# Shorter rows for the summing DMAs, fewer spilled partial sums and earlier table loads in a two-layer decoder trunk

## Chip, cores and metric

The kernel runs on one core of one Trainium2 chip. The metric is device time in microseconds (us) of one execution: the median of repeated runs. Beside the runs there is one execution under the hardware profiler, which gives the page and the trace that this document reads. Engines are named as the profile names them: PE is TensorE (matmuls; PEld its weight loads), DVE is VectorE, ACT is ScalarE, POOL is GpSimd, SP is SyncE, which issues most DMAs.

## The reference

A decoder trunk of two layers on 1024 tokens with a model width of 1024, all in float32. Each layer normalizes the tokens, projects them for four token mixers (latent attention with a rotary key, "a"; short gated convolution, "b"; causal pooling, "c"; sliding-window attention, "d"), normalizes each mixer's 256 outputs, joins them and projects them with `w_o` onto the residual; then comes a gated FFN of width 2816.

```python
for l in range(DEPTH):
    h = rmsnorm(x, attn_norm[l])
    proj = h @ w_in[l]
    (c_q, c_kv, k_r, g_b, g_c, u_conv, u_pool, q_sw, k_sw, v_sw) = jnp.split(proj, pts, axis=-1)
    y_a = mla_attention(c_q, c_kv, k_r, mla_q_norm[l], mla_kv_norm[l], w_uq[l], w_ukv[l], cos, sin)
    y_b = short_gated_conv(g_b, g_c, u_conv, conv_w[l])
    y_c = multiscale_pool(u_pool, pool_w[l], pool_scale[l])
    y_d = swa_sink_attention(q_sw, k_sw, v_sw, sinks[l], slopes)     # reshapes left out
    groups = jnp.stack([y_a, y_b, y_c, y_d], axis=2)
    gf = groups * lax.rsqrt(jnp.mean(groups * groups, axis=-1, keepdims=True) + RMS_EPS)
    mixed = gf.reshape(b, s, D_MIX) * mix_norm[l]
    x = x + mixed @ w_o[l]
    h2 = rmsnorm(x, ffn_norm[l])
    gate, up = jnp.split(h2 @ w_gate_up[l], 2, axis=-1)
    x = x + (jax.nn.silu(gate) * up) @ w_down[l]
return rmsnorm(x, final_norm)
```

## The kernel before

**Tiling.** Activations lie transposed: 128 channels on the partitions, 512 tokens (a half, `t` = 0 or 1) along the free dimension. Every float32 operand is split into a rounded high part and the rest (`split`, L285 to L293: a cast on ACT, L287 or L290, and a subtraction on DVE, L288 or L291), and a product is three matmuls (`mm3`, L270; all matmuls of this kind have line L276). A matmul of 128x512 starts every 0.227 us in the steady loops.

**Buffers.** `Slots` hands out 47 places of SBUF, each two halves of 128x512. A half is taken from the list of single free halves first, oldest first, else from the oldest free place. Which instruction reuses which half is thus fixed when the program is written out, and the reuse waits for the last reader, a DMA too. Small tiles have tags with their own buffers: `te` 2, `tn` 3, `tp` 3 (`tmp`, L186); PSUM has eight banks in four tags (`ps`, L180), and the tag "wide" goes round mm, s, mm, s, t, s, t.

**Order.** The framework orders the instructions of each engine at build time by its own model of the machine, so the trace does not show them strictly in the order of the code. Each engine then takes its list in order, and so does SP with the DMAs it issues.

**The stages of a layer.** First the projections: `project()` takes one weight tile (fetched one ahead by `ahead()`), makes two products of 24 matmuls, and steps the generator `dn_sums` twice. Window attention (`swa_unit`, transposes at L560), convolution and pooling run between them. Then come the query projections `cq`, `ckv`, and the rotary key, for which `rope_k` is loaded at L772 and multiplied on DVE, and `rope_q`, loaded at L790. Latent attention runs in eight steps over heads and halves (L1186 to L1240): `scores` (matmuls L890 to L892, exponentials L909 and L912), `mix_values` of the step before (transposes L944, matmuls L956, two small POOL memsets at L953), and 0, 3, 3, 3, 1, 1, 1, 1 parts of the output projection (`out_part`), which use mixers b, c and d alone.

**Partial sums.** A part (d, t) is output channels 128 d on and half t; OUT_PARTS goes through d = 0 to 7 with t = 1, then 0. `out_part` adds the residual, fetched by `fetch_x` (L1012). The first 13 parts are written to `xp` in HBM (L1000), and their half is freed; the last three stay. `out_last` reads the 13 back (L1084), adds mixer a's product (L1095), splits the result for the FFN, writes it to `xr` (L1098) and adds its squares to the norm `ss2` (L322, L324, L328).

**Sums of down-projection weights.** The FFN's down projection is done with seven products instead of eight (a Winograd form of Strassen's scheme), which needs sums of weight blocks. `dn_sums` makes them in HBM: per layer 16 plain copies (L159) and 16 DMAs that add onto them (L164, `accum_op`), 704 KB each, issued by POOL, each held back by `after_pe` until the last matmul written so far is done. The argument `max_dma_last_dim` bounds a DMA row.

**FFN start.** The first two gate/up columns are done plainly (`plain(f, u)`, u = 0 for t = 1): four products of 12 matmuls each, then gate times norm `r2[u]` on DVE, SiLU on ACT (L1292), times norm on POOL (L1293), and gate times up on DVE. The norm's matmul is L334 (`rnorm`: ACT L336 to L338, DVE L339 and L342). Between them `combine(j)` makes the sums of activations for the Strassen form, with four `tp` tiles (L1058, L1045, L1064, L1066) and four splits. From the third column on, `GateUp` loads a column's weights, sums blocks on POOL (L1128 to L1130), and splits them in `split1` to `split4`.

Of the kernel before, what the change touches and what calls it, by code (L numbers as in the profile page):

```python
# [33 lines left out]
HALVES = (1, 0)  # L34
OUT_PARTS = tuple((d, t) for d in range(NK) for t in HALVES)
N_U = 47
NG = NFF // 2


# [67 lines left out]
def trunk_kernel(ctx: ExitStack, tc: tile.TileContext, ins, out):  # L107
# [26 lines left out]
    act.preload_act_table_set("natural_log_exp_and_others")  # L134

    xs = dpool.tile([NK, P, S], F32, name="xs")
    xp = dpool.tile([NK, P, S], F32, name="xp")
    xr = dpool.tile([NK, P, S], F32, name="xr")
    ad = [dpool.tile([P, NG * HT], F32, name=f"ad{n}") for n in range(7)]

# [13 lines left out]
    def dn_sums(l):  # L154

        w = ins["w_dn"][l]
        for q, a, b in ((0, 2, 3), (2, 2, 0), (1, 0, 0), (3, 1, 1)):
            for m in range(NK // 2):
                after_pe(pool.dma_start(qd[q][m], qd[a][m] if q in (1, 3) else w[m, a]))  # L159
                yield  # L160
            for m in range(NK // 2):
                row = 4 * NG * P
                after_pe(
                    pool.dma_start(qd[q][m], w[m, b], accum_op=ALU.add, max_dma_last_dim=row)  # L164
                )
                yield

# [18 lines left out]
    def tmp(tag="te"):  # L186
        return tpool.tile([P, HT], F32, name=tag, tag=tag, bufs={"te": 2, "tn": 3, "tp": 3}[tag])
# [157 lines left out]
    def mul_to(o, a, b):  # L345
        dve.tensor_tensor(out=o, in0=a, in1=b, op=ALU.mult)  # L346
# [38 lines left out]
    for l in range(L):  # L385
# [344 lines left out]
            swa_some(2)  # L730
        R.free(sw)

        cq = [[None, None], [None, None]]
        sq_q = SumSq(2 * P)
        for m in range(2):
# [22 lines left out]
        for t in range(2):  # L758
            p = ps("mm")
            for k in range(NK):  # L760
                for n in range(2):
                    pe.matmul(
                        p,
                        wkr[:, k * P : (k + 1) * P],
                        R.ap(hh[k][t][n]),
                        start=k == 0 and n == 0,
                        stop=k == NK - 1 and n == 1,
                    )
            if t == 1:
                ahead()  # L770
            tk = F.half()
            sp.dma_start(F.ap(tk), ins["rope_k"][:, t * HT : (t + 1) * HT])  # L772
            mul_to(F.ap(tk), F.ap(tk), r_of(t))
            f = tmp()
            mul_to(f, p, F.ap(tk))
            F.free(tk)
            kr = half_split(f)
            p = ps("t")
            for n in range(2):
                pe.matmul(p, e_r, R.ap(kr[n]), start=n == 0, stop=n == 1)  # L780
                R.free(kr[n])
            for s in range(2):
                kb_[s][0][t], kb_[s][1][t] = R.half(), R.half()
                split(R.ap(kb_[s][0][t])[tl], R.ap(kb_[s][1][t])[tl], p[tl])
# [1 line left out]

        tq = []
        for t in range(2):
            s = F.half()
            sp.dma_start(F.ap(s), ins["rope_q"][:, t * HT : (t + 1) * HT])  # L790
            r = sq_q.rnorm(t)
            mul_to(F.ap(s), F.ap(s), F.ap(r))
            F.free(r)
            tq.append(s)
# [181 lines left out]

        x = [[None, None] for _ in range(NK)]

        def out_part(d, t, keep):
            next(sums, None)  # L980
            if t == HALVES[0]:
                out_w[:] = take()
# [11 lines left out]
            if t == HALVES[1]:  # L994
                ahead()
            dve.tensor_tensor(out=F.ap(s), in0=F.ap(s), in1=p, op=ALU.add)
            if keep:
                x[d][t] = s
            else:
                sp.dma_start(xp[d][:, t * HT : (t + 1) * HT], F.ap(s))  # L1000
                F.free(s)

        parts = deque(OUT_PARTS)
        coming = deque(OUT_PARTS)
# [7 lines left out]
                sp.dma_start(F.ap(s), src[:, t * HT : (t + 1) * HT])  # L1012
                residual.append(s)

        def out_some(n, keep=False):
            for _ in range(n):
                d, t = parts.popleft()
                out_part(d, t, keep)
                if d == NK - 1:
                    for g in "dcb":  # L1020
                        for c in range(2):
                            for s in mixed.pop((g, c, t)):
                                R.free(s)
# [54 lines left out]

        def out_last(t, ma):

            for d in range(NK):
                if x[d][t] is None:
                    x[d][t] = F.half()
                    sp.dma_start(F.ap(x[d][t]), xp[d][:, t * HT : (t + 1) * HT])  # L1084
            for d in range(NK):
                p = ps("wide")
                wh, wl = (R.ap2(i) for i in wa[d // 4])
# [157 lines left out]
            R.free(kb_[1][n][0])  # L1245
            R.free(va[n][1])
        ma0 = norm_a(0)
        out_some(len(parts), keep=True)
        out_last(HALVES[0], ma1)
        while ring:  # L1250
            ring_drop()
# [11 lines left out]
        def plain(f, u):  # L1263
# [4 lines left out]
            product(pg, blocks(w.s2, 0), hb[b[1]], False, True)  # L1268
            product(pu, blocks(w.s2, 1), hb[b[0]], True, False)
            product(pu, blocks(w.s1, 1), hb[b[1]], False, True)  # L1270
            if f == 0:
                r2.append(F.ap(ss2.rnorm(HALVES[u], tag="pv")))
            gate = tmp("tp")
            mul_to(gate, pg, r2[u])
            silu(gate, r2[u])
            acts[f].append(F.half())
            mul_to(F.ap(acts[f][u]), pu, gate)
            if u:
                for i in w.s1 + w.s2:
                    R.free_pair(i)  # L1280

        pending = None
        r2 = []

        def neg_mul(o, a, b):
            dve.scalar_tensor_tensor(  # L1286
# [106 lines left out]
        plain(0, 0)  # L1393
        combine(0)
        plain(1, 0)
        combine(1)
        plain(0, 1)
        w.sums()
        w.split1()
        w.split2()  # L1400
        combine(2)
        plain(1, 1)
        wn = GateUp(3)
        combine(3)
        for hl in hb[B12]:
            for i in hl:
                R.free(i)
# [306 lines left out]
```

## Time and profile before

| what | us |
|---|---|
| median of three runs | 2153.32 (2153.15 to 2154.82) |
| the profiled execution | 2153.01 |
| its span, first to last instruction | 2151.2 |
| DVE, ACT and POOL busy in the span | 1488.7, 989.8 and 430.2 |
| 0 to 340 us (layer 0, mixers): PE busy | 313.20 of 340 |
| 340 to 475 us (end of mixing, first FFN columns): PE busy | 129.76 of 135 |
| 475 to 520 us (third and fourth column): PE busy | 40.86 of 45 |
| 520 to 850 us (gate/up columns): PE busy | 330.00 of 330 |
| 850 to 1080 us (down projection): PE busy | 229.82 of 230 |
| 1080 to 1400, 1400 to 1540 and 1540 to 1580 us (the same in layer 1): PE busy | 300.58, 135.01 and 33.87 |

The granted PE clock is 0.986 over the span. A busy PE is not one at its peak, since matmuls overlap; what counts is the distance between their starts. On the DMA side, SP's queue moved 249.23 MB in 106,224 packets (33.2% of the time of the 16 DMA engines), and POOL's queue 46.19 MB in 5,664 packets (8.8%).

### The profile page before, as it was taken

Reading aid. Unit: us, or ns where it says so; the run is one execution under the profiler, and the core shown is the slowest. Engines: PE = TensorE matmul, PEld = TensorE weight load, DVE = VectorE, ACT = ScalarE, POOL = GpSimd, SP = SyncE. Lnnn points to the kernel's source line nnn. Section 1 sums busy time; section 2 is a strip of 40 time slices with the busy share of each in tenths; the row PEclk is TensorE's granted clock in tenths of the full one; section 3 lists DMA queues with packets and bytes.
Section 4 is the critical chain, followed back from the end, with each engine's and each line's share of the span. In section 5 each row is a group of like instructions: output and inputs, shape, how many; then the busy total and the mean of one; then the engine's idle time right before and its main releaser. Section 6 shows DMA issues by size and latency. Waiting matters only on the chain.

```text
span 2151.2 us, 26099 instructions
## 1 busy us (share of the span) xinstructions
PE 2073.8 (96%) x9418; PEld 1686.3 (78%) x9418; DVE 1488.7 (69%) x2417; ACT 989.8 (46%) x1716; POOL 430.2 (20%) x349
## 2 busy tenths in 40 slices
PE   8999889999999999999999998899999999999998
PEld 6777768687888888888888776677778888888887
DVE  6877958787666666655657888588876666675555
ACT  6446636663333334444433566366533333344442
POOL 0000000034535443000001000000353545410000
PEclk9999999999999999999999999999999999999999
DMA  4553453423232234866425444534223223267652
GB/s 176 138 153 100 125 152 124 162 80 111 85 127 85 107 113 142 291 239 201 149 86 144 125 106 133 138 121 149 82 90 122 94 103 116 81 222 267 214 183 89
DMA packets 112017, 297.08 MB, mean 138 GB/s; under 512 B 12672, under 2 KB 27008, under 8 KB 111376
## 3 DMA queue, kind: packets, MB, share of 16 engines
q1 hardware_dynamic: 106224, 249.23, 33.2%
q0 software_dynamic: 5664, 46.19, 8.8%
q8 instruction: 74, 1.21, 0.2%
q14 instruction: 55, 0.45, 0.1%
HBM read 231.40 MB, written 110.10 MB: 159 GB/s over the span
## 4 chain that ended last, share of the span: by engine, by line
PE 82%; DVE 7%; DMA 4%; ACT 3%; issue 2%; POOL 1%; SPq 0%; DVEq 0%; ACTq 0%; POOLq 0%
PE ps_mm L276 31%; PE ps_s L276 24%; PE ps_t L276 10%; PE ps_pv L276 8%; PE ps_pv L956 2%; PE ps_t L944 1%; DMA xp<-u 1%; DVE u L288 1%; PE ps_t L334 1%; PE ps_pv L572 1%; PE ps_s L890 1%; ACT u L287 1%; DVE u L291 1%; PE ps_t L560 1%; DVE u L328 1%
## 5 line engine op out<-in xcount | busy, mean ns | idle before, releaser
L276 PE MATMUL ps_mm<-u,u 128*128 128x512 f32 (+1 forms) x3394 | 839.3, 394 | 14.2 <-ACT u L290 11.1
L276 PEld LDWEIGHTS ps_mm<-u,u 128*128 128x128 f32 x3394 | 626.5, 191 | 142.1 <-ACT u L290 11.7
L276 PE MATMUL ps_s<-u,u 128*128 128x512 f32 x2652 | 632.3, 392 | 12.9 <-ACT u L287 5.9
L276 PEld LDWEIGHTS ps_s<-u,u 128*128 128x128 f32 x2652 | 498.5, 188 | 124.9 <-ACT u L287 6.8
L287 ACT CAST u<-u 128x1024 fp32r<-128x1024 f32 (+2 forms) x372 | 324.6, 897 | 428.8 <-PE ps_mm L276 130.5
L288 DVE TENSOR_TENSOR u<-u,u 128x1024 fp32r<-128x1024 f32 (+2 forms) x372 | 409.9, 1121 | 140.2 <-ACT u L287 115.5
L276 PE MATMUL ps_t<-u,u 128*128 128x512 f32 (+1 forms) x1146 | 260.3, 379 | 1.0 <-DVE u L1095 1.0
L276 PEld LDWEIGHTS ps_t<-u,u 128*128 128x128 f32 x1146 | 206.5, 188 | 43.6 <-issue 2.2
L1293 POOL TENSOR_TENSOR tp<-tp,u 128x512 f32<-128x512 f32 x88 | 132.7, 1507 | 398.3 <-ACT tp L1292 398.3
L276 PE MATMUL ps_pv<-u,u 128*128 128x512 f32 x744 | 176.4, 389 | 0.0
L276 PEld LDWEIGHTS ps_pv<-u,u 128*128 128x128 f32 x744 | 139.7, 188 | 29.0
L1292 ACT ACTIVATE tp<-tp 128x512 f32<-128x512 f32 x88 | 55.7, 633 | 148.1 <-DVE tp L346 147.7
L288 DVE TENSOR_TENSOR u<-ps_t,u 128x512 fp32r<-128x512 f32 (+4 forms) x136 | 78.3, 583 | 31.8 <-ACT u L287 30.8
L287 ACT CAST u<-ps_t 128x512 fp32r<-128x512 f32 (+4 forms) x136 | 67.0, 504 | 60.9 <-PE ps_t L944 30.6
L290 ACT ACTIVATE u<-u,par 128x512 fp32r<-128x512 f32 x100 | 70.1, 717 | 49.6 <-DVE u L1095 20.9
L1128 POOL TENSOR_TENSOR u<-u,u 128x512 f32<-128x512 f32 x40 | 62.6, 1565 | 128.1 <-PE ps_s L276 52.6
L346 DVE TENSOR_TENSOR tp<-tp,u 128x512 f32<-128x512 f32 x80 | 84.6, 1057 | 1.3
L1150 POOL TENSOR_TENSOR u<-u 128x512 f32<-128x512 f32 x40 | 69.0, 1725 | 58.2 <-DVE u L288 58.2
L291 DVE SCALAR_TENSOR_TENSOR u<-u,par,u 128x512 fp32r<-128x512 f32 x100 | 73.5, 760 | 8.6 <-ACT u L290 8.4
L164 POOL DMA_DIRECT2D qd<-in_w_dn x32 | 26.8, 942 | 260.8 <-PE ps_mm L276 80.0
L159 POOL DMA_DIRECT2D qd<-in_w_dn x16 | 7.9, 502 | 353.1 <-PE ps_t L276 289.6
L1286 DVE SCALAR_TENSOR_TENSOR u<-te,tp 128x512 f32<-128x512 f32 x40 | 29.8, 746 | 64.9 <-POOL tp L1293 64.9
(189 smaller groups left out, 2249.8 us busy)
## 6 DMA issues: line engine op xcount, KB each, us to landing
u<-in_w_gu SPq DMA_DIRECT2D x88, 512.0 KB, 3.6
ad<-u SPq DMA_DIRECT2D x154, 256.0 KB, 2.1
u<-ad SPq DMA_DIRECT2D x70, 512.0 KB, 5.3
qd<-in_w_dn POOLq DMA_DIRECT2D x48, 704.0 KB, 7.0
u<-qd SPq DMA_DIRECT2D x32, 512.0 KB, 4.9
u<-in_w_in SPq DMA_DIRECT2D x30, 512.0 KB, 3.5
u<-in_w_dn SPq DMA_DIRECT2D x24, 512.0 KB, 4.8
qd<-qd POOLq DMA_DIRECT2D x16, 704.0 KB, 4.7
```

The lines of the kernel that those rows point to most:

```text
L276: last_mm = pe.matmul(o, w, r, start=start and k == 0 and i == 0, stop=stop and k == n - 1 and i == 2, skip_group_check=again,)
L287: act.copy(hi, f)
L288: dve.tensor_tensor(out=lo, in0=f, in1=rd(hi), op=ALU.subtract)
L290: act.activation(hi, f, AF.Copy, scale=gain)
L291: dve.scalar_tensor_tensor(out=lo, in0=f, scalar=gain, in1=rd(hi), op0=ALU.mult, op1=ALU.subtract)
L346: dve.tensor_tensor(out=o, in0=a, in1=b, op=ALU.mult)
L956: pe.matmul(py[:, c0:], v_of(j, h), R.ap(s)[:, c0:], start=j == 0 and n == 0, stop=j == nj - 1 and n == 1,)
L1128: pool.tensor_tensor(out=F.ap(q + 1), in0=a21, in1=a22, op=ALU.add)
L1150: pool.tensor_tensor(out=q4, in0=q4, in1=F.ap(self.raw[1] + 1), op=ALU.add)
L1286: dve.scalar_tensor_tensor(out=o, in0=a, scalar=-1.0, in1=b, op0=ALU.mult, op1=ALU.mult)
L1292: last_silu = act.activation(g, g, AF.Silu)
L1293: pool.tensor_tensor(out=g, in0=g, in1=r, op=ALU.mult)
```

## The change

It does five things.

1. Every DMA of `dn_sums`, copies and sums alike, is given a row limit of `NG * P` = 1,408 where the sums had 5,632 and the copies none.
2. Only parts with d < 3 (`NSP`) go through `xp`, six of 16 instead of 13; parts with d = 3 to 7 stay in their halves until `out_last`.
3. The four loads of the rope tables are issued ahead of the first `cq` projection, into four halves that are held until used.
4. In the first two FFN columns the gate, SiLU and product of a half are no longer done behind each column's products: they are kept back in `waiting` and done for both columns together, in two steps (`plain_gates`, `plain_acts`) around `combine(1)` and `combine(3)`. The norm is taken with the second column (f == 1) instead of the first.
5. `split2` of the third column moves from before `combine(2)` to behind `combine(3)`.

```diff
+NSP = 3
...
-    xp = dpool.tile([NK, P, S], F32, name="xp")
+    xp = dpool.tile([NSP, P, S], F32, name="xp")
...
-                after_pe(pool.dma_start(qd[q][m], qd[a][m] if q in (1, 3) else w[m, a]))
+                src = qd[a][m] if q in (1, 3) else w[m, a]
+                after_pe(pool.dma_start(qd[q][m], src, max_dma_last_dim=NG * P))
                 yield
             for m in range(NK // 2):
-                row = 4 * NG * P
                 after_pe(
-                    pool.dma_start(qd[q][m], w[m, b], accum_op=ALU.add, max_dma_last_dim=row)
+                    pool.dma_start(
+                        qd[q][m], w[m, b], accum_op=ALU.add, max_dma_last_dim=NG * P
+                    )
                 )
                 yield
...
+        rope = []
+        for name in ("rope_k", "rope_q"):
+            for t in range(2):
+                rope.append(F.half())
+                sp.dma_start(F.ap(rope[-1]), ins[name][:, t * HT : (t + 1) * HT])
         cq = [[None, None], [None, None]]
...
-            tk = F.half()
-            sp.dma_start(F.ap(tk), ins["rope_k"][:, t * HT : (t + 1) * HT])
+            tk = rope[t]
...
-            s = F.half()
-            sp.dma_start(F.ap(s), ins["rope_q"][:, t * HT : (t + 1) * HT])
+            s = rope[2 + t]
...
-            if keep:
-                x[d][t] = s
-            else:
+            if d < NSP:
                 sp.dma_start(xp[d][:, t * HT : (t + 1) * HT], F.ap(s))
                 F.free(s)
+            else:
+                x[d][t] = s
...
-            for d in range(NK):
-                if x[d][t] is None:
-                    x[d][t] = F.half()
-                    sp.dma_start(F.ap(x[d][t]), xp[d][:, t * HT : (t + 1) * HT])
+            for d in range(NSP):
+                x[d][t] = F.half()
+                sp.dma_start(F.ap(x[d][t]), xp[d][:, t * HT : (t + 1) * HT])
...
-            if f == 0:
+            if f == 1:
                 r2.append(F.ap(ss2.rnorm(HALVES[u], tag="pv")))
-            gate = tmp("tp")
-            mul_to(gate, pg, r2[u])
-            silu(gate, r2[u])
-            acts[f].append(F.half())
-            mul_to(F.ap(acts[f][u]), pu, gate)
+            waiting.append((f, u, pg, pu))
...
+        def plain_gates():
+            for f, u, pg, pu in waiting:
+                gate = tmp("tp")
+                mul_to(gate, pg, r2[u])
+                silu(gate, r2[u])
+                gates.append((f, u, gate, pu))
+            waiting.clear()
+
+        def plain_acts():
+            for f, u, gate, pu in gates:
+                acts[f].append(F.half())
+                mul_to(F.ap(acts[f][u]), pu, gate)
+            gates.clear()
...
         plain(0, 0)
         combine(0)
         plain(1, 0)
+        plain_gates()
         combine(1)
+        plain_acts()
         plain(0, 1)
         w.sums()
         w.split1()
-        w.split2()
         combine(2)
         plain(1, 1)
         wn = GateUp(3)
+        plain_gates()
         combine(3)
+        w.split2()
+        plain_acts()
```

More of the change, by code (lines that the diff above doesn't have):

```diff
@@ L977, in trunk_kernel, with out_part @@
         x = [[None, None] for _ in range(NK)]
-        def out_part(d, t, keep):
+        def out_part(d, t):
             next(sums, None)
@@ L1247, in trunk_kernel @@
         ma0 = norm_a(0)
-        out_some(len(parts), keep=True)
+        out_some(len(parts))
         out_last(HALVES[0], ma1)
@@ L1282, in trunk_kernel @@
         pending = None
-        r2 = []
+        r2, waiting, gates = [], [], []
+        def plain_gates():
[10 more added lines that the diff above has]
+            gates.clear()
         def neg_mul(o, a, b):
```

4 lines of the change are left out of this document (2 added, 2 removed).

## The prediction

> **What bounds the kernel now.** I read the table of busy times first, then the list of who waits for whom on TensorE (PE), then the chain of waits and the timeline around the longest of those waits.
>
> ```profile
> PE 2073.8 (96%) x9418; PEld 1686.3 (78%) x9418; DVE 1488.7 (69%) x2417; ACT 989.8 (46%) x1716; POOL 430.2 (20%) x349
> ...
> PE   8999889999999999999999998899999999999998
> ```
>
> ```profile
> PE ps_s L890 <- ACT u L912: 18.5, 2, 10.6
> ...
> PE ps_s L276 <- ACT u L287: 5.9, 2, 3.8
> PE ps_t L560 <- DVE tp L549: 5.5, 5, 2.3
> PE ps_pv L334 <- DVE u L324: 4.0, 2, 3.2
> ```
>
> The second list gives the waiting matmul, what released it, us in total, times, and the longest: attention scores, first FFN columns, window attention beside the rope tables, and the norm ahead of the FFN. PE is busy 96% of 2151.2 us, so nothing can win more than the 77 us in which it is idle, and the steady loops leave nothing: from 520 to 850 us PE is busy 330.00 of 330 us. All that can be won lies in the mixers and at the start of the FFN. The longest wait there comes once per layer: an exponential (L912) that needs a buffer half which an xp write is still reading. The chain of waits in layer 0 shows it:
>
> ```profile
> 295.55 4.24 DMA xp<-u
> 299.81 0.33 SPq L1012
> 300.23 6.54 DMA xp<-u
> 306.80 0.47 ACT u L912 x2
> 307.31 0.79 PE ps_s L890
> ```
>
> Two writes follow one another, because the load between them (L1012, in order on SP's queue) reuses the half that the first write empties. PE stands 7.9 us. In layer 1 the same pair takes 9.25 and 3.02 us and PE stands 10.6 us. By the order of parts (three written after step 1, from 263 us; three after step 2, at 287.4, 295.6 and 300.2 us) these are parts (2,1) and (2,0). **They have d = 2, and the change still writes d < 3.** So keeping d >= 3 on chip does not touch this wait; only faster writes can.
>
> **Rows of the sums.** The two lines of POOL's DMA issues:
>
> ```profile
> L164 POOL DMA_DIRECT2D qd<-in_w_dn x32: 802/846/1179, 76.0 to 1378.9; - x32
> L159 POOL DMA_DIRECT2D qd<-in_w_dn x16: 486/490/541, 52.5 to 1178.3; - x16
> ```
>
> The packet records give 4096 rows of 5,632 B on that queue (32 accumulating DMAs x 128), median 441 ns, and 512 rows of 45,056 B (32 copies x 16), median 1902 ns. The limit of 5,632 thus counts bytes, and 1,408 makes 512 rows of every one of the 64 DMAs. Issue: (846 - 490) / (128 - 16) = 3.2 ns per row, so 2.07 us each, 32 x 1.58 + 32 x 1.22 = 90 us more on POOL. That lies beside idle: POOL is busy 24 us of the first 340, and nobody waited for its memsets (L953), the only other work there. If that cover fails, a memset comes 2 us later some twice per layer, 4 us.
>
> Time on the DMA engines: records on SP's queue cost 65 ns at 1,536 B and 84 ns at 2,048 B, so a plain row of 1,408 B costs about 61 ns, and 32 of them per engine 1.95 us against 1.90 now. An accumulating row of 5,632 B takes 441 ns, twice what the same line gives for a plain one (218 ns); at 1,408 B I estimate 2 x 61 = 122 ns, 4 x 122 = 490 against 441. The bounds: 110 ns (a quarter) and 441 ns (all of it a fixed price).
>
> What the short rows change is the turn. From 1358.5 to 1361.5 us, when an accumulating DMA and the xp write run together, about 15 records of 5,632 B and 14 of 2,048 B start in every half microsecond: one row against one row. The write has 8 rows per engine, 8 x (84 + 441) = 4.2 us of turns, against 8 x (84 + 122) = 1.6 us; and at 300.2 us it did not start for 1.7 us, until the accumulating rows already taken were through. I take 3.0 us for every xp write of the pair (median of the 26 now 3.1, least 2.0). Layer 0: 295.55 + 3.0, 0.44 to the next issue, + 3.0, + 0.5 to PE = 302.5 instead of 307.3, **4.8 us**. Layer 1 from 1356.34: 1363.3 instead of 1369.6, **6.3 us**. Sum 11; with 2.0 us per write 15; with nothing gained 0. What is late next is the weight load for the queries (L215), which SP issues behind the second write and which moves up with it.
>
> **The rope tables.**
>
> ```profile
> 163.59 0.33 SPq L772 DMA_DIRECT2D u<-in_rope_k  x1
> 170.41 0.69 DVE L346 TENSOR_TENSOR u<-u,u 128x512 f32<-128x512 f32 x1 [2.40 <-DMA u<-in_rope_k]
> 173.31 0.72 PE L560 MATMUL ps_t<-cst,tp 128*128 128x128 f32 x4 [2.25 <-DVE tp L549]
> ```
>
> VectorE (DVE) takes its work in order, so the window attention's tail waits behind the table, and PE for it: 2.25 us here, 2.36 in layer 1. Loaded before the two query projections (48 matmuls x 0.227 = 10.9 us each) the tables are there. The four loads pass the projection weights on SP's queue: 4 x 8 rows x 84 ns = 2.7 us, inside the 10.9 us by which weights are fetched ahead. They hold two of some 15 free slot places for that time. Gain 4 us; bounds 0 and 5.5.
>
> **Partial sums that stay.** 14 writes and 14 reads of 256 KB go, 28 x 0.33 us of SP's queue. No PE wait hangs on them: DVE waited 0.4 us for u<-xp in the whole run. Gain 0, bounds 0 and 2 (SP then issues the first w_gu loads earlier, L1122 at 396 us). The price is room. By the slot lists the sixth step's mixing (n = 6) now finds 4 to 5 free places; 5 halves kept leave about 2. Its pair of halves turns around in transposes 0.43 + cast 0.6 + subtraction 0.68 + two matmuls 0.45 = 2.2 us, so two places give 1.1 us a block against 0.89 us of PE: 8 x 0.2 = 1.6 us, part of it under the output products that PE mixes in. I charge 1 us for both layers; bounds 0 and 21 (one place: 8 x 1.3 x 2).
>
> **The first FFN columns.**
>
> ```profile
> 468.02 0.69 DVE L339 SCALAR_TENSOR_TENSOR tn<-ps_pv,tn 128x512 f32<-128x512 f32 x1 [5.30 <-ACT tn L338]
> 482.79 0.69 DVE L346 TENSOR_TENSOR u<-ps_mm,tp 128x512 f32<-128x512 f32 x1 [1.19 <-POOL tp L1293]
> 483.40 1.13 DVE L1045 SCALAR_TENSOR_TENSOR tp<-tp,te 128x512 f32<-128x512 f32 x1
> 485.23 0.72 PE L276 MATMUL ps_s<-u,u 128*128 128x512 f32 x1 [2.10 <-ACT u L287]
> ```
>
> DVE idles 5.3 us for the second norm, with combine(2) behind it; then combine(3) waits for a gate to leave its tp buffer, and PE for combine(3): 2.1 + 0.4 us in layer 0, 3.8 + 0.4 in layer 1. After the change the first norm follows plain(1, 0) and the second plain(1, 1), each 10.9 us later on PE. From 446 us on DVE owes 4 combines x 5.6, two norms x 1.4, eight gate and act products x 0.69 and two splits x 1.2 = 33 us, and PE needs combine(3) at 484: 38 us. So it fits if nothing idles, which gains all 6.7 us; it gains nothing if the idle time only moves; and there is a bad order, below (-32). No instruction is added. The 3.2 us before the first norm's matmul (L334) mostly stay, since the product behind it waits for a bank that DVE freed 0.5 us later. I take 3 us.
>
> **Sum:** 11 + 4 + 0 - 1 + 3 = 17 us off the profiled span of 2151.2, 2134.2; around it lie 1.8 us (profiled run 2153.0), and the median of the runs is 0.3 above that run: **2136 us**.
>
> **Rivals.** (1) **The wait for xp stays**, because several short rows pass in one turn: eight rows a turn, 8 x 122 = 1.0 us, make a write of 8 turns outlast the whole accumulating DMA of 32 x 122 = 3.9 us, just as now. For it: the 1.7 us at 300 us in which nothing of the write started. Against it: one against one at 1358 to 1361 us. Without the 11 us the time is 2147. The Trainium skill, DMA: Bandwidth & Descriptors, Queues, rings and completion order, says that an engine drains a whole packet, typically 9 to 17 descriptors, from one ring before it turns to the next, which speaks for this rival; SWDGE vs HWDGE vs iDMA on the same page prefers packets of at most 4096 B, which would be two such rows.
>
> (2) **Slower: the FFN start turns into a longer wait.** split2 of the third column now stands behind combine(3), and combine(3) behind gates that hold two of three tp buffers. If that order is kept on DVE: second norm's matmul at 475.5, its result 5.8 us later as now, gate to product 4.4, POOL's two sums in between 3.4, combine(3) 6.5, split2 2.3: 497.8, while PE wants the split at 479.1. That is 18.7 us per layer in place of 2.5 and 4.2, net +31 us; with the 15 us of the first two terms the time is 2169. For it: DVE has already waited in order, 5.3 us. Against: the trace shows work moved up past what isn't ready (combine(2)'s scalings at 460 us, before the norm's logarithm). It decides the sign from 13 us a layer.
>
> (3) **Room runs out** in the sixth step: 21 us instead of 1, 2156. For it: free places fall to about 2. Against: no PE wait of now names such a reuse except the xp one.
>
> That the change does not do what it says is in part my forecast: what stays on chip is not what PE waited for.
>
> **Chances.** Forecast 0.62, with its own range 2122 (15, 5, 7 and 2 us gained, and 2 of the 27.8 us in which ACT waits for projection weights) to 2146 (7 us from the first term alone); rival 1 0.16, rival 2 0.14, rival 3 0.08. About 0.2% (4.3 us) is what a measurement of this kernel can tell from no change. Faster: 0.61 + 0.11 + 0.02 = 0.74; same 0.01 + 0.05 + 0.03 + 0.03 = 0.12; slower 0.11 + 0.03 = 0.14. The range of 2122 to 2157 takes in the forecast, rivals 1 and 3, and leaves out most of rival 2.
>
> **What would show it.** Queue 0 with 32,768 records of 1,408 B; POOL's issues at 2 us; the wait of L890 for L912 still there, but at 3 us and 4 us instead of 7.9 and 10.6; no wait of L560 in the rope stage; 12 writes of xp. Wrong: if accumulating rows take far over 122 ns, if the wait for L912 is gone altogether (another buffer then), or if PE waits over 5 us for L287 or L288 behind the plain columns.

## The result, and the profile after

The changed kernel takes **2156.76 us** (median of 22 runs, 2151.72 to 2166.54), the kernel before 2152.91 (22 runs beside it). The ratio is 1.0023, with a 95% interval of 1.0013 to 1.0033: slower by 0.2%, where 0.8% faster was forecast. The profiled execution took 2159.47 us, 2.7 above its median; its span is 2157.7 us (before 2151.2). Line numbers are those of the changed kernel from here on: most are 5 to 22 higher (L276 is now L281, L890 L898, L912 L920, L560 L565). A profile of an experiment has the line numbers of its own kernel.

The page's busy times and the list of who waits for whom on PE (us in total, times, longest):

```profile
PE 2075.7 (96%) x9418; PEld 1685.9 (78%) x9418; DVE 1486.3 (69%) x2417; ACT 989.8 (46%) x1716; POOL 436.7 (20%) x349
...
PE   8999889998999999999999998899999999999997
```
```profile
PE ps_s L898 <- ACT u L920: 14.0, 4, 6.8
PE ps_mm L281 <- ACT u L295: 10.9, 3, 6.9
PE ps_s L281 <- ACT tn L1179: 7.5, 5, 2.2
PE ps_t L565 <- DVE tp L554: 6.6, 5, 2.5
PE ps_t L281 <- ACT u L292: 6.0, 4, 4.3
...
PE ps_s L898 <- ACT u L292: 3.4, 2, 2.4
```

Against the list before: the largest wait fell from 18.5 to 14.0 us, not to the forecast 7; the wait in the rope stage, forecast to go, rose from 5.5 to 6.6; and one is new: scores that wait for a cast of the query (L898 <- L292, 3.4). PE starts the same 9418 matmuls in both traces, so they can be numbered, and the distance from one to another can be compared stage by stage. This table accounts for 4.8 us of the 6.5 between the two spans (the stretches left out add up to +1.7). It sets one profile against one, and the medians lie only 3.9 us apart, so a row of a microsecond may be chance. The granted clock over the span, 0.986 before and 0.988 after, does not make the difference.

| stage (layers 0 and 1) | before, us | after, us | difference |
|---|---|---|---|
| window attention and rope stage | 87.6, 87.6 | 86.5, 87.6 | -1.1, +0.1 |
| first query weights and scores | 7.1, 5.3 | 7.9, 7.6 | +0.9, +2.3 |
| mixing up to the xp wait | 53.4, 56.3 | 55.6, 55.3 | +2.2, -0.9 |
| the xp wait | 15.2, 17.5 | 14.2, 13.6 | -1.0, -3.9 |
| sixth to eighth step of mixing | 46.3, 50.9 | 49.2, 53.9 | +2.9, +3.0 |
| end of mixing, FFN start | 105.2, 129.4 | 104.8, 130.0 | -0.4, +0.6 |
| FFN loop and all that follows | 629.6, 558.5 | 629.4, 558.7 | -0.1, +0.2 |

(The stages of a pair are not cut at the same matmul in both layers; before and after they are.) What was to win 17 us won 7, and 14 were lost at other places, most of them in the second, the third and the fifth row. (Of the third row's +2.2, 1.5 us are matmuls at a granted clock of 0.62 from 246 to 250 us. In the fifth row, layer 0 has 3.3 us at a clock of 0.50, from 375.3 to 378.6 us, which by that clock is about half of its +2.9; layer 1's +3.0 has none.)

**The xp wait.** The chain of waits around it in layers 0 and 1:

```profile
300.96 6.97 DMA xp<-u
307.93 0.02 issue
307.95 0.47 ACT u L920 x2
308.42 0.04 issue
308.46 0.79 PE ps_s L898
```
```profile
1364.52 7.54 DMA xp<-u
1372.06 0.02 issue
1372.09 0.47 ACT u L920 x2
```

It is the same wait for the same half. The first write of the pair took 3.3 and 3.4 us from issue to landing, near the forecast 3.0 (before 4.2 and 9.3). The second took 7.0 and 7.5 (before 6.5 and 3.0): it meets a whole accumulating DMA. The same two times stand in all seven kernels that have 512-row accumulating DMAs in the mixers: 3.1 to 3.4 us, then 6.7 to 7.5.

The DMA records say more. As before the change, SP issues a load of the residual just ahead of the write, on the same queue:

```profile
300.54 0.33 SPq L1020 DMA_DIRECT2D u<-in_xT  x1
300.96 1.07 SPq L1006 DMA_DIRECT2D xp<-u  x1
```

Records that start in each half microsecond, POOL's accumulating rows (1,408 B) and SP's queue (2,048 B, that load and that write):

```
from us   1,408 B   2,048 B
301.0        51        0
301.5        61        0
302.0        68        0
302.5        62        0
303.0        67        0
303.5        49        0
304.0        59        6
304.5        21       60
305.0        15       75
```

A row takes 131 ns, and 61 rows per half microsecond are 16 engines without a gap. The first 2,048-B record may be the load's or the write's; the records do not tell. It starts 3.8 us after the load's issue (3.5 in layer 1), where 1.0 us is enough with no row in the way (the load at 1365.65 us before). In the 2.8 and 2.5 us beyond that, 22 and 19 rows per engine went by; before the change, in layer 0, it was 2.4 rows of 5,632 B.

**New waits.** From the timeline: a projection weight in the rope stage, the small query weight in both layers, and an `ad` write in the FFN start. The bracket at the end is the idle time before the instruction and what ended it:

```profile
169.55 1.05 ACT L223 CAST u<-u 128x1024 fp32r<-128x1024 f32 x1 [4.50 <-DMA u<-in_w_in]
237.45 0.40 ACT L223 CAST vhi<-vraw 128x256 fp32r<-128x256 f32 x1 [2.53 <-DMA vraw<-in_w_uq]
482.43 0.69 DVE L344 SCALAR_TENSOR_TENSOR tn<-ps_pv,tn 128x512 f32<-128x512 f32 x1 [0.65 <-ACT tn L343]
506.21 1.99 ACT L292 CAST u<-u 128x1024 fp32r<-128x1024 f32 x2 [4.10 <-DMA ad<-u]
507.31 1.22 PE L281 MATMUL ps_t<-u,u 128*128 128x512 f32 x2 [4.33 <-ACT u L292]
1303.66 0.40 ACT L223 CAST vhi<-vraw 128x256 fp32r<-128x256 f32 x1 [3.93 <-DMA vraw<-in_w_uq]
```

DVE's wait for the second norm (5.30 us before) is 0.65 now, as forecast; but 24 us later a cast waits 4.10 us for an `ad` write that frees its buffer, and PE behind it 4.33.

POOL's groups, with the idle time before them:

```profile
L167 POOL DMA_DIRECT2D qd<-in_w_dn x32 | 33.3, 1041 | 289.5 <-issue 97.7
L163 POOL DMA_DIRECT2D qd<-in_w_dn x16 | 10.2, 644 | 340.6 <-PE ps_t L281 290.2
```

An issue costs 1.04 and 0.64 us (before 0.85 and 0.49), not 2.07. But POOL now stands 97.7 us in 14 waits that no semaphore ends: beside the projections the second accumulating DMA of a pair is issued 7 to 9 us after the first, where it was 0.6 us. The four of layer 0's mixer start at 288.9, 297.4, 307.5 and 318.8 us (before 286.1, 290.1, 295.5, 316.9). The trace does not name what POOL waits for; that it is room for descriptors in a ring, as some of the expectations below have it, no run shows.

### The profile page after: what moved, and what is told of

Read it like the earlier page. It is cut to its first block, busy times and chain, and to the rows that moved or that the text cites. A ratio compares the mean times of both kernels' runs of the same rounds, so it can differ in the third digit from the quotient of the medians.

```text
span 2157.7 us, 26038 instructions
## 1 busy us (share of the span) xinstructions
PE 2075.7 (96%) x9418; PEld 1685.9 (78%) x9418; DVE 1486.3 (69%) x2417; ACT 989.8 (46%) x1716; POOL 436.7 (20%) x349
## 4 chain that ended last, share of the span: by engine, by line
PE 83%; DVE 7%; DMA 4%; ACT 4%; issue 1%; POOL 1%; SPq 0%; DVEq 0%; ACTq 0%; POOLq 0%
PE ps_mm L281 31%; PE ps_s L281 26%; PE ps_t L281 10%; PE ps_pv L281 8%; PE ps_pv L964 2%; ACT u L292 1%; PE ps_t L952 1%; DVE u L293 1%; DMA u<-in_w_gu 1%; DMA u<-in_w_in 1%; PE ps_t L339 1%; PE ps_t L565 1%; PE ps_pv L577 1%; DMA xp<-u 1%; DMA u<-xp 1%
## 5 line engine op out<-in xcount | busy, mean ns | idle before, releaser
L281 PE MATMUL ps_mm<-u,u 128*128 128x512 f32 (+1 forms) x3394 | 838.4, 394 | 14.2 <-ACT u L295 10.9
L281 PEld LDWEIGHTS ps_mm<-u,u 128*128 128x128 f32 x3394 | 625.5, 190 | 144.3 <-ACT u L295 11.6
L281 PE MATMUL ps_s<-u,u 128*128 128x512 f32 x2652 | 629.8, 391 | 12.1 <-ACT tn L1179 7.5
L281 PEld LDWEIGHTS ps_s<-u,u 128*128 128x128 f32 x2652 | 498.1, 188 | 123.2 <-ACT tn L1179 9.6
L292 ACT CAST u<-u 128x1024 fp32r<-128x1024 f32 (+2 forms) x372 | 325.2, 897 | 444.1 <-PE ps_mm L281 143.4
L281 PE MATMUL ps_t<-u,u 128*128 128x512 f32 (+1 forms) x1146 | 260.8, 379 | 6.5 <-ACT u L292 5.3
L281 PEld LDWEIGHTS ps_t<-u,u 128*128 128x128 f32 x1146 | 207.1, 189 | 49.4 <-ACT u L292 6.1
L281 PE MATMUL ps_pv<-u,u 128*128 128x512 f32 x744 | 176.6, 389 | 0.0
L281 PEld LDWEIGHTS ps_pv<-u,u 128*128 128x128 f32 x744 | 139.6, 188 | 29.3 <-DVE te L1473 0.3
L292 ACT CAST u<-ps_t 128x512 fp32r<-128x512 f32 (+4 forms) x136 | 67.0, 505 | 61.5 <-PE ps_t L952 33.1
L167 POOL DMA_DIRECT2D qd<-in_w_dn x32 | 33.3, 1041 | 289.5 <-issue 97.7
L224 DVE TENSOR_TENSOR u<-u,u 128x1024 fp32r<-128x1024 f32 (+1 forms) x46 | 51.8, 1129 | 42.2 <-ACT u L223 21.9
L163 POOL DMA_DIRECT2D qd<-in_w_dn x16 | 10.2, 644 | 340.6 <-PE ps_t L281 290.2
```

The source lines that it names most:

```text
L224: dve.tensor_tensor(out=lo[:, :n], in0=raw[:, :n], in1=rd(hi[:, :n]), op=ALU.subtract)
L281: last_mm = pe.matmul(o, w, r, start=start and k == 0 and i == 0, stop=stop and k == n - 1 and i == 2, skip_group_check=again,)
L292: act.copy(hi, f)
```

## The experiments

Eighteen kernels, each timed against the kernel before in the same session. Its median moved between 2150.7 and 2154.5, so kernels of different sessions are compared by their ratios; 0.1% is 2.2 us.

| label | what it is | median, us | ratio to before (95%) |
|---|---|---|---|
| u_rows | changed, rows undone | 2164.73 | 1.0056 (1.0042 to 1.0070) |
| u_keep | changed, kept halves undone | 2148.58 | 0.9990 (0.9978 to 1.0002) |
| u_rope | changed, early tables undone | 2155.61 | 1.0011 (0.9997 to 1.0025) |
| u_ffn | changed, FFN start undone | 2155.81 | 1.0011 (1.0000 to 1.0022) |
| u_sums | changed, short rows for copies only | 2159.91 | 1.0030 (1.0014 to 1.0045) |
| room | u_keep with places withheld | 2159.88 | 1.0037 (1.0019 to 1.0055) |
| o_rows | before + both kinds of short rows | 2150.29 | 0.9986 (0.9970 to 1.0003) |
| o_copies | before + short copies | 2146.96 | 0.9973 (0.9960 to 0.9986) |
| o_sums | before + short accumulating rows | 2158.87 | 1.0028 (1.0010 to 1.0046) |
| o_2816 | before + short copies, sums of 2,816 B | 2144.83 | 0.9962 (0.9949 to 0.9974) |
| k_2816 | o_2816 + early tables and FFN start | 2150.55 | 0.9985 (0.9971 to 0.9999) |
| no_sums | before + short copies, no accumulating DMAs | 2122.15 | 0.9864 (0.9839 to 0.9888) |
| late_long | before, all these DMAs in the FFN loop | 2141.42 | 0.9946 (0.9925 to 0.9967) |
| late_short | the same with short rows | 2185.66 | 1.0148 (1.0122 to 1.0175) |
| late_after | changed, all in the FFN loop | 2192.31 | 1.0187 (1.0160 to 1.0214) |
| late2 | late_long, placed behind POOL's work | 2196.81 | 1.0212 (1.0192 to 1.0233) |
| half_long | before, the mixer's eight in the FFN loop | 2129.58 | 0.9905 (0.9889 to 0.9922) |
| **half_late** | o_2816 with the mixer's eight in the FFN loop | **2125.39** | **0.9878 (0.9856 to 0.9900)** |

### One part undone at a time

Each of these takes one numbered part of the change back to the text of the kernel before (u_ffn: parts 4 and 5).

> The changed kernel with the DMA rows as they were (copies without a limit, sums in rows of 5,632 B); the three other edits stay. Theory (short accumulating rows hold a DMA engine until their DMA is through, so other transfers start later): the two new PE waits before the first scores of a mixer (1.2 us at 237 us with 1.5 us of throttled clock behind it, 2.7 us at 1302 us) go, 4.5 to 5.5 us; the gap of the xp write returns from 6.4 to about 8.1 us and from 7.0 to about 10.7 us, 5.4 us; about 2157 us, as the changed kernel. Rival (short rows only help the xp write): the early waits stay, 2162 us. Rival (the short rows are the whole loss): 2152 us or less.

> The changed kernel with the partial sums as they were (all but those of the last pieces written to xp and read back); rows, rope tables and FFN start stay changed. Theory (kept halves and the transfers that no longer stand between the weight loads move work into the last steps of the mixer): the 2 to 4 us that the changed kernel loses around 372 us and the 2.5 us around 1406 to 1442 us go: about 2151 us. Rival (keeping costs nothing, these waits belong to other edits): 2157 us.

> The changed kernel with the rope tables loaded where they were. Theory (their early loading won nothing, since the tail of window attention waits 2.0 and 2.7 us in the changed kernel too): 2156 to 2158 us. Rival (it won the forecast 4 us, and other edits took them away at another place): 2161 us, with waits of the transposes ahead of window attention's end of over 4 us.

> The changed kernel with the FFN start as it was (gates and products at once, second split before combine(3)). Theory (deferring wins 5.6 and 4.4 us ahead of the plain products and loses 5.2 and 4.2 us behind them, at 480 to 507 us and 1543 to 1570 us, because combos and the next weight load come later): 2156 to 2157 us, with both losses gone from behind and both gains gone from ahead. Rival (the FFN start is the whole loss): 2152 us. Rival (it is a net gain): 2160 us.

By the ratios, undoing the kept halves wins 7 us, which brings the kernel level with the one before: they make the change a loss. Undoing the rows costs 7 us: they are a gain. Undoing the early tables or the FFN start wins 2.6 us each, with intervals that overlap the changed kernel's; neither is a gain of 3 or 4. The four together give +5, which is the 1.0023 of the changed kernel. In u_rows the early waits went as the theory said (gaps of 0.4 us at both query weights), and the xp gaps rose from 6.4 and 7.0 to 10.9 and 7.9 us; the median rose more than any of the theories had it.

### Room, or the order of transfers?

```diff
             out_some(pieces[n])
+            for _ in range({3: 2, 6: 1}.get(n, 0)):
+                held.append(F.s.places.popleft())
...
         out_some(len(parts), keep=True)
+        F.s.places.extend(held)
```

> The changed kernel with the partial sums as they were, and in the mixers as many slot places withheld as the kept halves take (two from the fourth step on, a third from the seventh, given back ahead of the last products): free places 5, 5, 2, 10, 14 in the last five blocks, as in the changed kernel, and every transfer of xp as before the change. Theory (room): what keeping costs, 8 us, comes back: 2155 to 2157 us. Rival (the cost is the changed order of transfers and work, not room): 2149 us. In between: both.

2159.9 us, 10 more than u_keep by the ratios: withholding places brings the loss back, with every xp transfer in place. Listing the free places as the program is written out gives 7, 7, 4, 13, 17 for the last five blocks of u_keep, and 5, 5, 2, 10, 14 here and in the changed kernel. The stage shows it too, in all twenty traces at once: the sixth to eighth step of layer 0 takes 47.8 to 49.2 us in the seven kernels with kept halves or withheld places, and 45.0 to 46.5 in all others, the kernel before among them; in layer 1 81.9 to 85.2 against 79.0 to 80.5 (over a slightly longer stretch than in the table above). Two of the seven, the changed kernel and room, have 3.4 us at half the granted clock in layer 0's stretch, room in layer 1's too; the other five have none, so the clock is not the cause, but part of room's 10 us may be clock.

No single wait carries it. In layer 1's stretch it is the matmuls that mix the values (L964): PE's pauses over 0.1 us ahead of them add up to 2.7 to 3.5 us in the six kernels with kept halves, to 1.8 in room (where another 2.2 go to a weight's cast) and to 0.9 at most in all others. The PE waits of that stretch in the changed kernel and in the one before (L956 there):

```profile
PE ps_pv L964 <- DVE u L293: 1.3, 2, 1.0
PE ps_pv L964 <- ACT u L292: 1.3, 3, 0.9
PE ps_pv L964 <- DVE u L980: 0.6, 1, 0.6
```
```profile
PE ps_pv L956 <- DVE u L288: 0.6, 1, 0.6
PE ps_mm L276 <- ACT u L218: 0.2, 1, 0.2
```

The clearest line of layer 0, from the changed kernel's sixth step:

```profile
373.27 0.68 PE L964 MATMUL ps_pv<-u,u 128*128 128x512 f32 x2 [1.15 <-DVE u L293]
```

### The two kinds of rows apart

The kernel before with the limits of the changed kernel is o_rows. Against it, o_sums takes the copies' limit away, o_copies sets the sums' limit to `4 * NG * P` again (u_sums does that in the changed kernel), and o_2816 to twice the short one:

```diff
             pool.dma_start(
-                qd[q][m], w[m, b], accum_op=ALU.add, max_dma_last_dim=NG * P
+                qd[q][m], w[m, b], accum_op=ALU.add, max_dma_last_dim=2 * NG * P
             )
```

> The kernel before with the short DMA rows alone. Theory (the edits add up: short rows -8, kept sums +8, rope tables +1, FFN start +1): 2146 to 2148 us, faster than both kernels. Rival (short rows win only beside another of the edits): 2153 us.

> The kernel before with short rows for the accumulating DMAs alone, the 32 copies long as before. Theory (the gap of the xp write is set by the accumulating rows): as with both, 2146 to 2149 us, xp gaps of 5 to 7 us. Rival (the copies of 45,056 B hold the rope tables and the weight loads): 2150 to 2152 us, with waits of 2 to 3 us left in the rope stage.

> The kernel before with short rows for the 32 copies alone, accumulating DMAs in rows of 5,632 B as before. Theory (short copies are what wins, short accumulating rows with long copies cost 6 us): 2144 to 2148 us. Rival (neither wins alone): 2153 to 2157 us.

> The changed kernel with accumulating rows of 5,632 B again, copies in short rows and the other edits as changed. Theory (short accumulating rows lose 3 us even beside short copies, by the wait for ring room and by holding the small weight loads, against their gain on the xp write): 2152 to 2155 us, the gaps at the first query weights back at 0.4 us, those of the xp write at 8 us and more. Rival (short sums win once tables are loaded ahead and halves are kept, as the 8 us of undoing both kinds of rows suggest): 2160 us or more.

> The kernel before with short copies and accumulating rows of 2,816 B. Theory (what short sums lose goes with the number of rows: 256 leave room in the ring for the next DMA): 2146 to 2148 us, POOL's wait for room gone or under 2 us, a row of 220 to 260 ns. Rival (any row under 5,632 B loses): 2150 us.

Short **copies** win 5 to 6 us by themselves: the rope stage's gaps fall from 2.4 and 2.4 us to 1.1 and 0.2 with the tables loaded late, as before. Short **accumulating** rows of 1,408 B do not. Without short copies they lose 6 us (o_sums, where theory and rival both expected a gain). Beside them they lose 3 (o_rows against o_copies), with intervals that overlap, and 1.4 and 2.6 us of the rope wait are left; o_rows met neither its 2148 nor its 2153 us. In the changed kernel taking them away costs 1.5 us (u_sums), with intervals that overlap: its theory of 2152 to 2155 us is not met, and its rival of 2160 us is by the median and not by the ratio. They shorten the xp gaps (5.2 to 7.0 us in all seven kernels that have them in the mixers, 7.4 to 10.9 with longer rows, 2,816 B among them), and lengthen those at the small query weights (1.2 to 3.1 us, against 0.4 with longer rows). Rows of 2,816 B are level with 5,632 or a little better, 2144.8 us.

The short ones also make POOL wait. Of the kernels with 512 rows per accumulating DMA, o_rows:

```profile
POOL qd L167 <- issue: 96.3, 14, 9.7
```

With 256 and 128 rows that line is not in the list, though an issue of 256 rows takes nearly as long as one of 512 (medians 0.92 and 1.04 us, and 0.85 for 128). The mean in this line of o_2816, 1024 ns, is raised by the twelve issues that another one follows at once, 1.2 us each:

```profile
L167 POOL DMA_DIRECT2D qd<-in_w_dn x32 | 29.0, 1024 | 255.0 <-PE ps_mm L281 78.6
```

> The changed kernel with the partial sums as they were and accumulating rows of 2,816 B; short copies, early rope tables and the FFN start stay changed. Theory (what is left of the change wins nothing beside such rows, since short copies already took the wait for the tables): 2143 to 2146 us, as the kernel before with those rows alone. Rival (the early tables and the deferred gates win 2 us each): 2141 us.

2150.6 us, 5 more than o_2816 by the ratios, with intervals that just overlap. Early tables and the FFN start, added to better rows, lose; beside accumulating rows of 1,408 B they cost 1 us, which is inside the intervals (u_keep against o_rows). The rope stage of layer 0 is 86.8 us with early tables and 84.2 without:

```profile
169.28 1.05 ACT L223 CAST u<-u 128x1024 fp32r<-128x1024 f32 x1 [5.40 <-DMA u<-in_w_in]
...
173.04 0.33 PE L565 MATMUL ps_t<-cst,tp 128*128 128x128 f32 x1 [2.75 <-DVE tp L554]
```

ACT waits 5.4 us for a projection weight, DVE and PE behind it. This is the line of the changed kernel (4.50 at 169.55 us). All eight kernels that load the tables early have it, with 2.3 to 6.1 us, and none of the twelve others. Four halves held are two places fewer for the weight loads, and SP's waits show it. In k_2816 SP issues that weight load at 162.59 us, once a matmul of window attention (L516) has freed a place; in o_2816 the rope_k load waits for the same matmul and goes at 162.46:

```profile
SPq L215 <- PE ps_s L516: 7.5, 1, 7.5
```
```profile
SPq L777 <- PE ps_s L516: 3.7, 1, 3.7
```

### What the accumulating DMAs cost at all

> The kernel before with copies in short rows and no accumulating DMA at all (the second addend of the four combined down weights is left out of the computation; nothing else is). It bounds what any row size can win. Theory (accumulating DMAs delay the xp write and the small weight load): the gaps of the xp write fall from 8.1 and 10.7 us to 3 or 4 us and the time to 2138 to 2143 us. Rival (the two xp writes and the loads beside them are late by themselves): gaps of 6 us or more stay, 2147 us.

2122.15 us: 30 us go, of which short copies alone give 5 to 6 (o_copies), so the accumulating DMAs cost some 24. Both xp gaps fall to 0.17 us, with all 26 xp writes still in place, and the writes of the pair land in 2.0 to 2.3 us. The xp write was never slow by itself. The list of PE waits no longer has the line of the exponential, and begins:

```profile
PE ps_mm L276 <- ACT u L290: 11.3, 3, 7.2
PE ps_s L276 <- ACT u L287: 4.5, 2, 2.3
PE ps_mm L276 <- DVE u L823: 3.6, 4, 1.6
```

### The DMAs at another place

half_late and half_long move the eight of the mixer, by this edit (on o_2816 and on the kernel before):

```diff
 def out_part(d, t, keep):
-    next(sums, None)
...
 for f in range(2, NFF):
...
+            next(sums, None)
             pc = ps("ac")
             product(pc, blocks(w.sq, 1), hb[N1])
```

The three late kernels also take the two steps of `project()` away and add a second one ahead of `gate1`. late2 puts the two steps behind `silu(gate, r2[0])` and `wn.sum4()` instead, and lets `after_pe` wait for the last matmul of the pair of columns before.

> The kernel before with its copies and accumulating DMAs (rows as before) moved from the projections and mixers into the FFN loop, two issues per pair of columns from the third on. Theory (they cost the mixers 30 us, as the run without accumulating DMAs showed, and the loop, whose DMA engines are 28% busy and whose PE has no idle time, can hide them): 2122 to 2130 us. Rival (in the loop POOL waits with each issue for PE, and the gate products behind it and the weight loads come late): 2140 us or more.

> The same with rows of 1,408 B for both. Theory (away from the mixers the row size has little to decide): within 2 us of the one with long rows. Rival (the longer issues, 1.0 us for 0.85 and 0.65 for 0.49, and the wait for ring room of 7 to 9 us between two accumulating DMAs hold POOL's gate products): 5 us or more slower than with long rows.

> The changed kernel with the DMAs moved into the FFN loop in the same way. Theory (kept halves take room, whatever the DMAs do): 8 to 11 us slower than the kernel before with the same move and short rows. Rival (kept halves cost only where accumulating DMAs hold the transfers that free a place): the same time within 3 us.

> The kernel before with its copies and accumulating DMAs, rows as before, in the FFN loop, each issued behind a POOL operation of the same pair of columns and paced by the last matmul of the pair before, which PE has passed by then. Theory (the 19 us that the first placing lost against no accumulating DMAs at all come from POOL waiting up to 6.1 us for PE with gate products behind it): 2122 to 2130 us. Rival (they come from the DMAs holding the weight loads of the loop): 2138 to 2143 us, as the first placing.

Moving all 32 of a layer wins 10.5 us with long rows, and loses 34 with short ones. The 19 us lost against no_sums lie in the FFN loop (354.7 us for 345.0 in layer 0, 353.1 for 344.8 in layer 1). Whether they come from POOL waiting for PE, as the theory had it, late2 does not settle: POOL's waits for PE ahead of these DMAs fell from 81 us in late_long to 5, but the kernel is 55 us slower, since the new placing has losses of its own and met neither expectation. Its PE waits, and one of them in the timeline:

```profile
PE ps_pv L281 <- ACT tn L1174: 37.1, 8, 6.8
PE ps_s L281 <- ACT tn L1174: 17.4, 15, 2.7
```
```profile
517.69 1.04 ACT L292 CAST u<-u 128x1024 fp32r<-128x1024 f32 x1 [7.48 <-DMA ad<-u]
520.49 1.04 ACT L292 CAST u<-u 128x1024 fp32r<-128x1024 f32 x1 [1.76 <-DMA ad<-u]
521.82 3.45 DVE L293 TENSOR_TENSOR u<-u,u 128x1024 fp32r<-128x1024 f32 x2 [8.05 <-DMA ad<-u]
...
522.59 0.79 PE L281 MATMUL ps_pv<-u,u 128*128 128x512 f32 x1 [4.91 <-ACT tn L1174]
```

The copy out of PSUM (L1174) stands behind a cast that waits for a write (`ad`) to free its place, as the casts of the mixer wait for the xp write. The waits for L1174 add up to 54.5 us, against 15.1 in late_long, and ACT's waits for `ad` writes to 114 us, against 58 in late_long and 21 in the kernel before. In late2 fourteen of the 64 issues follow the one before by 0.5 us; in late_long none comes sooner than 5.0 us. That the writes are late because of accumulating rows is the likely reading, by the mixer's case and by the 345 us of a loop without these DMAs; it wasn't tried by itself in the loop. late_after is 6.7 us slower than late_short. It has the early tables and the new FFN start too, but 5.2 of the 6.7 us lie in the sixth to eighth step (47.8 and 82.7 us against 45.5 and 79.8): kept halves cost even where no accumulating DMA is near.

> The kernel before with short copies and accumulating rows of 2,816 B, and of the 32 DMAs per layer only the eight of the mixer (four copies, four accumulating) moved into the FFN loop, one issue per pair of columns; those beside the projections stay. Theory (the accumulating DMAs beside the xp write cost 7.9 and 7.8 us, each of them in the loop some 0.6 us, by the first placing): the xp gaps fall to under 1 us and the time to 2131 to 2137 us. Rival (in the loop they hold the ad writes that free places, as in the second placing, 1 to 1.5 us each): 2138 to 2143 us.

> The kernel before with only the eight DMAs of each mixer moved into the FFN loop, all rows as before. Theory (the move does the most, the rows beside the projections win the rope stage's 2.2 and 1.3 us and little else): 2128 to 2134 us, xp gaps under 1 us, rope gaps of 2 us. Rival (long rows in the loop cost as much as the move wins): 2140 us or more.

Moving only the mixer's eight per layer, one issue per pair of columns, wins 20 us with old rows and 26 with short copies and sums of 2,816 B, by the ratios: **2125.4 us, 1.2% faster than the kernel before, some 1.4% than the changed one**. Both xp gaps are 0.17 us, and the loop gives back 1.6 and 1.2 us, where 0.6 for each accumulating DMA, 2.4 a layer, were expected. Its PE waits are nearly those of no_sums:

```profile
PE ps_mm L281 <- ACT u L295: 11.2, 3, 7.1
PE ps_s L281 <- ACT tn L1176: 6.8, 8, 1.6
PE ps_s L281 <- ACT u L292: 4.2, 2, 2.1
```

## Why the prediction was wrong, point by point

**What bounds the kernel** held: all that moved lies in the mixers and at the FFN start, the loops stayed within 0.2 us, and the wait for xp was indeed untouched by keeping d >= 3.

**The step that turned the sign is the price of room: "I charge 1 us for both layers".** It came from a turnaround of 1.1 us a block against 0.89 us of PE, and took part of that as covered by the output products mixed in. Measured: +2.9 and +3.0 us in the sixth to eighth step, 7 us in all by undoing it, 10 by withholding as many places without any other edit. It is not covered: in layer 1 PE stands 3.2 us ahead of the mixing matmuls, where it stood 0.6. The mechanism (about two free places in the sixth step) was the right one, and rival 3 had it; but its 21 us were too many, and that its time, 2156, was met is chance: two other terms fell short at the same time.

**Rows: "one row against one row" was wrong, and it is the largest error in size.** The xp wait gave 4.9 us (1.0 and 3.9) instead of 11. The rule was read from 3 us in layer 1 with rows of 5,632 B. In these, only 87 of the 256 records of the write and of the load ahead of it on the queue started, so the turns may have been the load's; the sum has no term for that load. With 1,408 B, 22 and 19 rows per engine went by before the first record of load or write. This is rival 1's mechanism, at half the loss that it gave: the first write of each pair had the forecast's 3 us, the second did not. The Trainium skill, DMA: Bandwidth & Descriptors, Queues, rings and completion order, has a DMA engine drain a packet of typically 9 to 17 descriptors from one ring before it turns to the next. The trace's 22 and 19 rows are somewhat more than that. By that rule alone the xp term would have been 0, as in rival 1; it was 4.9.

**And the rows had a price that the sum did not have.** The estimate of a row, 122 ns, was near (131 ns, so 4.2 us an engine for one DMA, where the long rows take 3.5). But with 512 rows POOL issues the second DMA of a pair 7 to 9 us after the first; that DMA then ran beside the load of the small query weights, and the first scores came 0.9 and 2.3 us later. The forecast counted POOL's issue time as hidden, which it was; it had no term for where the moved DMAs would land. (Its 3.2 ns of issue per row came from setting an accumulating DMA against a plain one. Between accumulating DMAs of 128, 256 and 512 rows it is about 0.5 ns.)

**Rope tables: "Gain 4 us" was 1**, and by undoing it a loss. The wait for the table went, and a wait for a weight of the same length took its place. The sum had said of the loads that they "hold two of some 15 free slot places for that time" and gave that no price. What shortens the rope wait with the tables loaded late are the short copies, all but about a microsecond of it in o_copies and less beside short accumulating rows (o_rows). They stood in the forecast only as a row cost: it had read the copies' records of 45,056 B, but not that two such copies are issued at 162.9 and 163.4 us, beside the table's load at 163.59.

**FFN start: "I take 3 us" was 0** (-0.4 and +0.6). The named idle time, 5.30 us of DVE, went as forecast; the condition "it gains nothing if the idle time only moves" came true, with a cast waiting 4.1 us for an `ad` write and PE 4.3. Rival 2's 18.7 us a layer did not happen: no wait there passes 4.4 us.

**Of the signs to look for**: 12 writes of xp, as said; sums in 16,384 records of 1,408 B, but the copies in records of 4,224 B (three rows each, or two); POOL's issue half of what was said; the L920 wait at 6.3 and 6.8 us instead of 3 and 4; the rope wait still there.

What stays open: how the missing places delay the casts and subtractions ahead of the mixing matmuls (the waits name the engine, not the place); what POOL waits for between two DMAs of 512 rows; and whether short accumulating rows beside short copies lose on the kernel before (3 us) and win in the changed one (1.5 us), since both are inside the intervals.

## What to carry to other kernels

Ask what a wait costs with its cause taken away altogether before pricing a milder form of it: with short copies and no accumulating DMAs 30 us went, the best rows won 8 of these, and moving a quarter of the DMAs, rows as they were, won 20. An edit that holds buffers (kept results, tables loaded early) is paid for where the free list is shortest, even if it removes transfers; withholding the same number of buffers in the kernel without that edit measures the price alone. Where buffers are handed out in turn, a slow write is a late buffer, so look for casts that wait for a DMA out of their own buffer.

## What the runs showed of the hardware

- A plain copy's rows are joined in one record (three of 1,408 B, 164 ns); accumulating rows are not (131 ns each, 234 ns at 2,816 B, 441 ns at 5,632 B).
- POOL's issue of an accumulating DMA takes 0.85 us for 128 rows, 0.92 for 256 and 1.04 for 512 (medians); with 512, and in these runs only then, the next one waits, up to 10.3 us (late_short).
- With no accumulating row in the way, a load on SP's queue has its first record 1.0 us after its issue (at 1365.65 us before); beside an accumulating DMA of 512 rows it took 3.8 and 3.5 us (at 300.54 and 1364.11 us after).
- Runs of one kernel lay up to 15 us apart: the changed kernel 2151.7 to 2166.5 us in 22 runs, o_rows 2145.6 to 2157.0 in 12, half_late 2123.5 to 2128.6 in four. One profile places a wait, but a difference of 3 us needs the medians.
